# Cached pages split on VectorE instead of ScalarE and VectorE, two pairs ahead, in a hybrid decoder step

## The chip, the cores and the metric

The kernel runs on one core of a Trainium2 chip. The core has a matrix engine (TensorE, PE in the profile; PEld is its loading of stationary weights), VectorE (DVE), ScalarE (ACT), GpSimd (POOL) and a queue engine (SP); POOL and SP issue DMAs here. Each engine works through its own list of instructions in order and waits at an instruction until what it needs is there. The metric is the device time of one execution in microseconds (us).

## The reference, cut to what matters

A trunk of two layers is run for a prompt of 512 tokens and for 8 sample sequences of one token. In each layer a projection feeds three mixers, then comes an output projection and a gated feed-forward part. One mixer is latent attention. For the sample sequences it reads a cache of 4096 past positions, 32 pages of 128 positions for each sequence, through a page table. The keys are not cached: each page of 128 latent vectors (256 wide) is multiplied with the 256 x 512 key weights, and each of the 8 heads' 64 columns is normalised by its root mean square.

```python
def mla_attend_sample(q_nope, q_rope, c_all, kr_all, w_uk, w_uv, k_nope_g):
    k_nope = rms_norm(jnp.einsum('blc,chd->blhd', c_all, w_uk), k_nope_g)
    s = (jnp.einsum('bqhd,blhd->bhql', q_nope, k_nope)
         + jnp.einsum('bqhr,blr->bhql', q_rope, kr_all)).astype(jnp.float32) * SM_SCALE
...
    pr = jax.nn.softmax(s, axis=-1).astype(c_all.dtype)
    o_lat = jnp.einsum('bhql,blc->bqhc', pr, c_all)
    return jnp.einsum('bqhc,chd->bqhd', o_lat, w_uv)
```

The prompt's own attention and the gated recurrence are computed at the same time as the pages.

## The kernel before, in words

Products keep float32 accuracy with a faster matrix format (float32r): an operand x is split into a high half, x rounded to float32r, and a low half, x minus the high half, and the product is the sum of three matmuls (high by high, high by low, low by high). `split` (L291) makes both halves: the high one by a copy on ScalarE, unless its argument `e` names another engine, and the low one by a subtraction on VectorE.

Each layer has a stretch in which the 256 pages of the 8 sequences are worked through: `sample` (L1275), a generator that yields once per page. Two pages make a pair. `load` (L1285) requests the two pages of a pair by two DMAs on SP's queue into one tile, ct. `halve` (L1296) splits the tile into cth and ctl; the halves are written in another order of blocks (k, g, t) than they are read (g, k, t), so the output is strided. The product of a page is 12 matmuls (four groups of three, with the key weights' halves wkh and wkl) into two of four PSUM banks (tile pool pk); ScalarE squares the two results into ksq and copies 8 columns of scores (tile s), and VectorE sums the squares by head (ss, L1449). Before the pages of pair pr, the code calls load(pr + NCT) with NCT = 3 and halve(pr + 1); before the first page it loads three pairs and splits pair 0. At the end of each sequence `chain` turns scores into probabilities and multiplies them with the pages in their natural order (nat), which POOL gathers from memory (L1335). POOL also gathers the rotary keys (kr, L1314).

`mixers` (L857) runs the streams beside the pages: at each page it takes a step of the convolution and recurrence (`first_streams`) and one of the prompt's attention (`attend`), at fixed rates, so that the instructions of all of them stand interleaved on each engine, in an order that is fixed when the program is written. In `attend`, scores are computed on PE in one step, their row maximum (pm) on VectorE one step later, the exponential on ScalarE one step after that, and the transposes on PE two steps after VectorE's normalisation. The first pages are set up within `z_phase`, before the last tile of the input projection (z) is taken from its banks and before VectorE's ra, an input of the last normalisation of keys. SBUF tiles of this size come from one pool of 68 buffers (tag t, L245); a new tile waits for the last reader of its buffer.

Of the kernel before, what the change touches and what calls it, by code (L numbers as in the profile page):

```python
# [71 lines left out]
PLAIN = (0, 1, 2, 3)  # L72
NNAT = 6
KEEP = 3
NCT = 3


def constants():
# [150 lines left out]
class Trunk:  # L229
# [1045 lines left out]
    def sample(self):  # L1275
        nc, a, l = self.nc, self.a, self.l
# [8 lines left out]
        def load(i):  # L1285
            if i >= npair or i in raw or i in halves:
                return
            r = self.t("ct")
            for pgi in range(2):
                n = 2 * i + pgi  # L1290
                reg = nc.sync.value_load(self.idx[0:1, n:n + 1], min_val=0, max_val=POOL_N - 1)
                nc.sync.dma_start(out=r[:, pgi * 256:(pgi + 1) * 256],
                                  in_=a['ct'][l][bass.ds(reg, 1)].rearrange("o p c -> (o p) c"))
            raw[i] = r

        def halve(i):  # L1296
            if i >= npair or i in halves:
                return
            load(i)
            r = raw.pop(i)  # L1300
            hi, lo = self.t("cth", F32R), self.t("ctl", F32R)

            v = [x[:, 0:512].rearrange("p (k g t) -> p g k t", k=4, g=2) for x in (hi, lo)]
            self.split(v[0], v[1], r[:, 0:512].rearrange("p (g k t) -> p g k t", k=4, g=2))
            halves[i] = (hi, lo)

        def load_kr(b, gqs):
            if b >= NB:
                return
            if b not in krs:  # L1310
                krs[b] = self.w("kr")
            k = krs[b]
            for gq in gqs:
                nc.gpsimd.indirect_dma_start(  # L1314
                    out=k[:, gq * P:(gq + 1) * P], out_offset=None, in_=a['krt'].rearrange("l n c -> (l n) c"),
                    in_offset=bass.IndirectOffsetOnAxis(ap=self.idx4[:, 8 * b + gq:8 * b + gq + 1], axis=0),
                    element_offset=l * POOL_N * ROPE * PG)

        def set_q(b):
            if b >= NB:  # L1320
                return
            q = self.qabs[:, 0:128].rearrange("p (k b h) -> p k b h", k=2, b=8)[:, :, b, :]
            o = 256 + 264 * (b % 2)
            hv = self.wkh.rearrange("p (k c) -> p k c", k=2)[:, :, o:o + 8]
            lv = self.wkl.rearrange("p (k c) -> p k c", k=2)[:, :, o:o + 8]
            self.split(hv, lv, q)
# [6 lines left out]
        def load_nat(b, i):  # L1333
            n = b * NPG // 2 + i
            nc.gpsimd.indirect_dma_start(  # L1335
                out=nat(b, i)[:, 0:512], out_offset=None, in_=a['cn'].rearrange("l n c -> (l n) c"),
                in_offset=bass.IndirectOffsetOnAxis(ap=self.idx2[:, n:n + 1], axis=0),
                element_offset=l * POOL_N * PG * LAT)
# [77 lines left out]

        for i in range(NCT):
            load(i)
        load_kr(0, range(8))
        set_q(0)  # L1420
        halve(0)
        chains = [self.own_scores()]
        yield
        for b in range(NB):
            s1, ss, sr = self.s("s1"), self.s("ss"), self.s("sr")
            w0 = 256 + 8 * (b % 2)
            qo = 256 if b % 2 else 0
            ko = 0 if b % 2 else 8
            for t in range(NPG):
                n = b * NPG + t  # L1430
                pr = n // 2
                if t % 2 == 0:
                    load(pr + NCT)
                    halve(pr + 1)
                    cur = halves.pop(pr)
                sq = self.t("ksq")
                for hf in range(2):
                    ps = self.pk("k")
                    c0, cn = ((0, 256), (w0, 264))[hf]
                    for kt in range(2):  # L1440
                        o = (2 * kt + t % 2) * P
                        for i, (cx, wx) in enumerate(((cur[0], self.wkh), (cur[0], self.wkl), (cur[1], self.wkh))):
                            self.mm(ps[:, 0:cn], cx[:, o:o + P], wx[:, 528 * kt + c0:528 * kt + c0 + cn],
                                    kt == 0 and i == 0, kt == 1 and i == 2)
                    k0 = ko if hf else 0
                    self.act(sq[:, 256 * hf:256 * hf + 256], ps[:, k0:k0 + 256], AF.Square)
                    if hf:
                        self.act(s1[:, 8 * t:8 * t + 8], ps[:, qo:qo + 8], AF.Copy)
                nc.vector.tensor_reduce(out=ss[:, 8 * t:8 * t + 8], in_=sq[:, 0:512].rearrange("p (h d) -> p h d", d=64),  # L1449
                                        axis=AX.X, op=ALU.add)  # L1450
                if t == 2:
                    set_q(b + 1)
                if b == 0 and t in (6, 8):
                    nc.gpsimd.memset(self.pp2[t == 8][:, 0:1024], 0.0)
                if b == NB - 1 and t == LAST:
                    self.nat_last = [self.t("natl") for _ in range(NPG // 2)]
                    todo.extend((b, i) for i in range(NPG // 2))
                if t == 10:
                    k = krs.pop(b)[:, 0:1024].rearrange("p (x g c) -> p x g c", x=2, g=4)
                    psr = self.ps("sr")  # L1460
                    for gq in range(4):
                        self.mm(psr[32 * gq:32 * gq + 32, 0:256], self.bd[:, 32 * b:32 * b + 32], k[:, :, gq, :])
                    del k
                    srt = self.t("srt")
                    self.act(srt[:, 0:512].rearrange("p (x h d) -> p x h d", x=4, h=2),
                             psr[:, 0:256].rearrange("p (x h d) -> p x h d", x=4, h=1).to_broadcast([P, 4, 2, 64]), AF.Copy)
                if 14 <= t < 22:
                    load_kr(b + 1, [t - 14])
                if t == 12:
                    psr = self.ps("sr")  # L1470
                    for x in range(4):
                        nc.tensor.transpose(psr[:, x * P:(x + 1) * P], srt[:, x * P:(x + 1) * P], self.c(C_ID))
                    src = psr.rearrange("p (x e c g h) -> p x e c g h", x=2, e=2, c=8, g=2)
                    dst = sr.rearrange("p (x c e h) -> p x e c h", x=2, e=2, c=8)
                    for hh in range(2):
                        r = slice(64 * hh, 64 * hh + 64)
                        for x in range(2):
                            self.act(dst[r, x], src[r, x, :, :, hh, :], AF.Copy)
                    psr = srt = src = None
                self.page = n  # L1480
                for _ in range(NPOP):
                    if todo:
                        load_nat(*todo.pop(0))
                chains = [g for g in chains if next(g, self) is not self]
                yield
            if b == 0:
                assert self.sn is not None
            chains.append(chain(b, s1, ss, sr))
# [526 lines left out]
```

## Time and profile before

| what | value |
|---|---|
| time, median of 3 runs | 2197.75 us (2195.72 to 2198.5) |
| time of the profiled execution | 2197.29 us |
| its span, first to last instruction | 2195.2 us |
| busy: PE, PEld, DVE, ACT, POOL | 98%, 92%, 80%, 59%, 20% of the span |
| granted TensorE clock, mean | 0.998 of full speed |

The busy share is that of one execution. Ends of matmuls are modelled, so a stall of PE can be partly hidden in a matmul that looks long; waits of the weight loads are listed beside those of the matmuls. The page stretches lie at about 170 to 700 us (first layer) and 1240 to 1780 us (second layer) of the span.

### The profile page before, as it was taken

The numbers are of one execution on the slowest core, as the hardware profiler recorded it, in microseconds if no ns is written. First come the engines' busy times: TensorE is split into PE (matmuls) and PEld (weight loads), VectorE is DVE, ScalarE is ACT, GpSimd is POOL, SyncE is SP. The second block draws the span as 40 slices with busy tenths as digits, with TensorE's granted clock in tenths as the row PEclk, the third lists the DMA queues.
The fourth block names the chain that finished last, engine by engine and source line by source line (L and its number), as shares of the span: only waits on it lengthen the run. The fifth ranks groups of instructions, "written<-read, shape, count | busy, mean of one in ns | idle before, by whom it ended". The sixth has DMA issues, their size and how long they took to land.

```text
span 2195.2 us, 50795 instructions
## 1 busy us (share of the span) xinstructions
PE 2147.8 (98%) x18330; PEld 2013.3 (92%) x18330; DVE 1760.1 (80%) x3673; ACT 1291.1 (59%) x3364; POOL 436.6 (20%) x470
## 2 busy tenths in 40 slices
PE   8999999999999999999999999999999999999999
PEld 8998888888888999999999988888888889999999
DVE  7778889877676699889777788897776857998895
ACT  6667767677674554444356677676776745444341
POOL 0004334333362000000001134234333610000000
PEclk9999999999999999999999999999999999999999
DMA  5213445453574423333233134445445733333232
GB/s 183 99 49 107 116 129 146 129 148 119 165 227 142 136 84 106 106 110 98 77 103 105 59 96 138 124 134 151 135 130 163 237 120 117 110 106 102 90 104 78
DMA packets 149484, 267.72 MB, mean 122 GB/s; under 512 B 22833, under 2 KB 103090, under 8 KB 149234
## 3 DMA queue, kind: packets, MB, share of 16 engines
q1 hardware_dynamic: 121778, 178.47, 25.7%
q0 software_dynamic: 24576, 75.52, 11.9%
q10 hardware_dynamic: 2880, 10.49, 1.5%
q8 instruction: 145, 2.38, 0.4%
q14 instruction: 105, 0.86, 0.1%
HBM read 259.86 MB, written 4.54 MB: 120 GB/s over the span
## 4 chain that ended last, share of the span: by engine, by line
PE 77%; DVE 12%; ACT 7%; issue 3%; DMA 1%; SPq 0%; POOL 0%; DVEq 0%; POOLq 0%; ACTq 0%
PE k L268 29%; PE b L268 17%; PE pr L268 17%; PE pv L268 3%; PE wo L268 3%; ACT ry L283 2%; PE sc L268 2%; DVE ss L1449 1%; DVE wl L271 1%; PE ov L268 1%; DVE ctl L271 1%; PE gr L268 1%; DVE sl L271 1%; ACT wh L283 1%; DVE z L271 1%
## 5 line engine op out<-in xcount | busy, mean ns | idle before, releaser
L268 PE MATMUL k<-wkh,cth 128*128 128x256 f32 (+1 forms) x2048 | 619.7, 303 | 3.4 <-ACT ksq L283 1.9
L268 PE MATMUL k<-wkh,ctl 128*128 128x256 f32 (+1 forms) x2048 | 581.5, 284 | 7.4 <-DVE ctl L271 7.3
L268 PE MATMUL k<-wkl,cth 128*128 128x256 f32 (+1 forms) x2048 | 578.0, 282 | 0.0
L283 ACT ACTIVATE ksq<-k 128x256 f32<-128x256 f32 x1024 | 378.8, 388 | 273.2 <-PE k L268 269.3
L1449 DVE TENSOR_REDUCE ss<-ksq 128x8 f32<-128x512 f32 x512 | 347.6, 681 | 169.4 <-ACT ksq L283 165.9
L268 PEld LDWEIGHTS k<-wkh,cth 128*128 128x128 f32 x2048 | 385.8, 188 | 54.9 <-ACT s L283 27.4
L268 PEld LDWEIGHTS k<-wkh,ctl 128*128 128x128 f32 x2048 | 385.3, 188 | 12.6 <-DVE ctl L271 11.8
L268 PEld LDWEIGHTS k<-wkl,cth 128*128 128x128 f32 x2048 | 386.1, 189 | 6.5 <-issue 3.8
L1335 POOL DMA_INDIRECT nat<-in_cn,idx x224 | 231.2, 1032 | 517.7 <-PE pv L268 389.9
L268 PE MATMUL b<-fh,wd 128*128 128x260 f32 x1408 | 232.0, 282 | 1.1 <-ACT fh L283 1.1
L271 DVE TENSOR_TENSOR ctl<-ct,cth 128x512 fp32r<-128x512 f32 x256 | 175.8, 687 | 27.4 <-ACT cth L283 26.8
L268 PEld LDWEIGHTS b<-fh,wd 128*128 128x128 f32 x1408 | 195.3, 188 | 1.5 <-ACT fh L283 1.5
L283 ACT ACTIVATE swh<-sw 128x512 fp32r<-128x512 f32 x144 | 90.8, 631 | 133.6 <-DVE sw L271 129.7
L283 ACT ACTIVATE cth<-ct 128x512 fp32r<-128x512 f32 x256 | 163.2, 637 | 1.2 <-DMA ct<-in_ct 1.1
L268 PE MATMUL b<-fl,wd 128*128 128x260 f32 x704 | 141.8, 283 | 0.5 <-DVE fl L271 0.5
L1314 POOL DMA_INDIRECT kr<-in_krt,idx x128 | 132.4, 1034 | 38.6 <-issue 36.4
L268 PE MATMUL b<-hh,wh 128*128 128x260 f32 x640 | 130.7, 285 | 8.0 <-ACT wh L283 7.2
L268 PE MATMUL b<-hl,wh 128*128 128x260 f32 x640 | 130.1, 285 | 0.2 <-DVE hl L274 0.2
L268 PE MATMUL b<-hh,wl 128*128 128x260 f32 x640 | 129.8, 284 | 0.0
L271 DVE TENSOR_TENSOR x<-x,b 128x260 f32<-128x260 f32 x224 | 84.8, 420 | 33.5 <-PE b L268 32.4
L268 PEld LDWEIGHTS b<-fl,wd 128*128 128x128 f32 x704 | 108.4, 188 | 0.9 <-DVE fl L271 0.9
L268 PEld LDWEIGHTS b<-hh,wh 128*128 128x128 f32 x640 | 99.7, 190 | 8.7 <-ACT wh L283 7.2
(346 smaller groups left out, 5209.2 us busy)
## 6 DMA issues: line engine op xcount, KB each, us to landing
ct<-in_ct SPq DMA_DIRECT2D x512, 128.0 KB
wg<-in_w_gate SPq DMA_DIRECT2D x44, 512.0 KB
wu<-in_w_up SPq DMA_DIRECT2D x44, 512.0 KB
wr<-in_w_in SPq DMA_DIRECT2D x40, 512.0 KB
wdr<-in_w_down SPq DMA_DIRECT2D x96, 192.0 KB
wr<-in_w_out ACTq DMA_DIRECT2D x20, 512.0 KB
wdr<-in_w_down SPq DMA_DIRECT2D x16, 256.0 KB
nat<-in_cn,idx POOLq DMA_INDIRECT x224, 3.5
```

The lines of the kernel that those rows point to most:

```text
L268: self.nc.tensor.matmul(out, lhsT, rhs, start=start, stop=stop)
L271: (e or self.nc.vector).tensor_tensor(out=out, in0=a, in1=b, op=op)
L283: self.nc.scalar.activation(out=out, in_=a, func=f, **k)
L1314: nc.gpsimd.indirect_dma_start(out=k[:, gq * P:(gq + 1) * P], out_offset=None, in_=a['krt'].rearrange("l n c -> (l n) c"), in_offset=bass. ...
L1335: nc.gpsimd.indirect_dma_start(out=nat(b, i)[:, 0:512], out_offset=None, in_=a['cn'].rearrange("l n c -> (l n) c"), in_offset=bass.Indirec ...
L1449: nc.vector.tensor_reduce(out=ss[:, 8 * t:8 * t + 8], in_=sq[:, 0:512].rearrange("p (h d) -> p h d", d=64), axis=AX.X, op=ALU.add)
```

## The change

The high halves of the pages are made by VectorE's cast in place of ScalarE's copy; pairs are split two ahead instead of one, and loaded one pair earlier.

```diff
-NCT = 3
+NCT = 4
...
             v = [x[:, 0:512].rearrange("p (k g t) -> p g k t", k=4, g=2) for x in (hi, lo)]
-            self.split(v[0], v[1], r[:, 0:512].rearrange("p (g k t) -> p g k t", k=4, g=2))
+            self.split(v[0], v[1], r[:, 0:512].rearrange("p (g k t) -> p g k t", k=4, g=2), nc.vector)
             halves[i] = (hi, lo)
...
         halve(0)
+        halve(1)
         chains = [self.own_scores()]
...
                 if t % 2 == 0:
                     load(pr + NCT)
-                    halve(pr + 1)
+                    halve(pr + 2)
                     cur = halves.pop(pr)
```

## Rows read from the trace of the kernel before

**Rows 1.** The page's chain that ended last, shares of the span by line.

```profile
PE k L268 29%; PE b L268 17%; PE pr L268 17%; PE pv L268 3%; PE wo L268 3%; ACT ry L283 2%; PE sc L268 2%; DVE ss L1449 1%; DVE wl L271 1%; PE ov L268 1%; DVE ctl L271 1%; PE gr L268 1%; DVE sl L271 1%; ACT wh L283 1%; DVE z L271 1%
```

**Rows 2.** Windows: length, then busy us (instructions) of PE, PEld, DVE, ACT, POOL.

```profile
170.00:300.00 130.00, 122.47 (x987) 110.73 (x988) 107.13 (x225) 93.96 (x308) 51.39 (x60) 1.00 0.42 123
300.00:400.00 100.00, 98.99 (x962) 86.05 (x962) 93.80 (x227) 69.53 (x226) 26.82 (x27) 1.00 0.41 120
...
1240.00:1360.00 120.00, 112.90 (x909) 104.36 (x908) 100.92 (x219) 82.03 (x263) 38.21 (x48) 1.00 0.34 97
1360.00:1500.00 140.00, 138.44 (x1293) 120.66 (x1296) 124.70 (x287) 99.61 (x321) 52.54 (x54) 1.00 0.46 135
...
sum 1070.00, PE 1045.58 PEld 923.35 DVE 847.11 ACT 742.82 POOL 412.01; mean PE 149.37 PEld 131.91 DVE 121.02 ACT 106.12 POOL 58.86
```

**Rows 3.** Waits of the whole span: us in total, times, longest.

```profile
POOL nat L1335 <- PE pv L268: 389.9, 79, 22.6
...
DVE ctl L271 <- ACT cth L283: 26.8, 40, 3.0
...
PEld k L268 <- DVE ctl L271: 11.8, 22, 1.0
...
PE k L268 <- DVE ctl L271: 7.3, 17, 0.8
PEld stat L268 <- DVE sl L271: 7.2, 9, 1.7
...
PEld mx L1365 <- DVE sa L271: 2.3, 2, 1.2
...
PE k L268 <- ACT ksq L283: 1.9, 4, 0.5
```

**Rows 4.** Timeline around one wait: start, length, in brackets the idle time before.

```profile
190.28 0.28 PE L268 MATMUL k<-wkl,cth 128*128 128x256 f32 x1
...
191.32 0.39 PE L268 MATMUL k<-wkh,ctl 128*128 128x256 f32 x1 [0.76 <-DVE ctl L271]
```

**Rows 5.** Groups by form: busy us, mean ns of one, idle time before them.

```profile
L271 DVE TENSOR_TENSOR ctl<-ct,cth 128x512 fp32r<-128x512 f32 x256 | 175.8, 687 | 27.4 <-ACT cth L283 26.8 <-PE k L268 0.2
...
L283 ACT ACTIVATE cth<-ct 128x512 fp32r<-128x512 f32 x256 | 163.2, 637 | 1.2 <-DMA ct<-in_ct 1.1
...
L387 DVE CAST wh<-wr 128x1024 fp32r<-128x1024 f32 x4 | 2.8, 690 | 3.0 <-DMA wr<-in_w_in 3.0
```

**Rows 6.** Timeline of DVE, two instructions in a row.

```profile
145.79 0.43 DVE L278 TENSOR_SCALAR f<-z 128x512 f32<-128x512 f32 x1
146.14 0.42 DVE L280 TENSOR_SCALAR f<-z 128x512 f32<-128x512 f32 x1
```

**Rows 7.** Timeline of the start of the second layer's pages.

```profile
1254.88 6.01 SPq L1292 DMA_DIRECT2D ct<-in_ct  x6
...
1258.78 1.01 POOL L1314 DMA_INDIRECT kr<-in_krt,idx  x1 [0.30 <-issue]
...
1259.53 0.63 ACT L283 ACTIVATE cth<-ct 128x512 fp32r<-128x512 f32 x1 [1.09 <-DMA ct<-in_ct]
1259.68 0.42 DVE L660 COPY kT<-kr 64x520 f32<-64x520 f32 x1
...
1260.72 0.67 DVE L271 TENSOR_TENSOR ctl<-ct,cth 128x512 fp32r<-128x512 f32 x1
...
1261.32 0.75 DVE L271 TENSOR_TENSOR z<-b,rstd 128x260 f32<-128x260 f32 x2
...
1262.44 0.85 ACT L283 ACTIVATE ry<-stat,consts 128x260 f32<-128x260 f32 x2 [2.27 <-DVE ra L280]
...
1265.05 0.61 ACT L283 ACTIVATE cth<-ct 128x512 fp32r<-128x512 f32 x1
1265.57 0.64 ACT L283 ACTIVATE ksq<-k 128x256 f32<-128x256 f32 x2
...
1265.98 0.49 PE L268 MATMUL sc<-kT,ev 128*128 128x128 f32 x2 [1.64 <-ACT ksq L283]
```

## The prediction

> **What bounds the kernel now.** I read the chain that ended last first, then the busy times of the two stretches that the change touches, then the waits by engine, and last the timeline around single waits. The chain is mostly PE's, and its largest line is the k product of the sample pages, 29% of the span [rows 1]: the two page stretches, 170 to 700 us and 1240 to 1780 us, are PE's, and what the change is worth is read there. In them PE is busy 1045.58 of 1070 us, DVE 847.11, ACT 742.82 [rows 2]. The reader is to see how uneven DVE is: from 300 to 400 us it has 6.2 us free in 100, from 1360 to 1500 us 15.3 in 140, from 170 to 300 us 22.9 in 130.
>
> PE's own stalls in those stretches are few, and the one that this change aims at leads the list: the k product waits for a page pair's low half [rows 3]. Its size is read in two ways, 7.3 us in 17 waits by the matmuls and 11.8 us in 22 by the weight loads. Matmul ends are modelled, so I check one wait: the ctl matmul started 1.04 us after the matmul before it [rows 4], where neighbours in this stream start 0.12 us apart (at 1.04 the loss is 0.92); PE's row put it at 0.76, the weight load's at 0.96. So the weight loads' sum is nearer: 11.8 x 0.92 / 0.96 = 11.3 us.
>
> Why the low half is late: it is made one pair (1070 us / 256 pairs = 4.2 us) before its use, on DVE, behind whatever the streams have queued there and behind ACT's copy, for which DVE stood 26.8 us in 40 waits [rows 3].
>
> **The change part by part.** *Removed from ACT:* 256 copies of 637 ns, 163.2 us of busy time [rows 5]. ACT was free 327 us of the 1070, so this pays only where PE waits for ACT: 1.9 us of k product behind ACT's squares [rows 3]. Ends 0 and 1.9; I take 0.9, because a lighter ACT still has the same squares in front of each bank.
>
> *Added to DVE:* 256 casts of 128x512. No such cast with the strided output stands in the trace. From below: a plain 128x512 TENSOR_SCALAR on DVE lasts 0.43 us, and the next instruction starts 0.35 us after it [rows 6]; the plain cast of twice the elements lasts 0.690 us, little more than the 0.687 us of a two-operand instruction of half its elements [rows 5]. From above: the low half's own instruction, same strides and two inputs, starts its follower 0.60 us later (1260.72 to 1261.32) [rows 7]. I take 0.35, because the cast has one input and its nearest kin in operation is the cast row; 0.60 stays as the other end. So DVE gets 256 x 0.35 = 89.6 us and gets back the 26.8 us for which it stood behind ACT's copy, since both halves now come from its own queue: 847 + 90 - 27 = 910 of 1070, 85%.
>
> [...]
>
> *What DVE's extra work hides behind:* its own free time. At 24 casts per 100 us, 300 to 400 us needs 8.4 us and has 6.2: 2.2 us short. 1360 to 1500 us needs 11.7 and has 15.3; 170 to 300 needs 10.9 and has 22.9; 1240 to 1360 needs 10.0 and has 19.1 [rows 2]. Free time that lies in the wrong place doesn't help a queue that is late for a moment, so I take 3.5 us as PE's loss: the 2.2, and about 1.3 for shorter crowded spots. Ends: 0, since streams place a consumer one or two page steps after its producer, and 8. If the cover is gone, what is late next is DVE's pm (the row maximum that ACT's exponential waits for), then ACT's squares behind it in its queue, then the banks of the k product.
>
> *Moved:* the split goes from one pair ahead to two. A low half then has 8.4 us of program between making and use, against the longest wait of 1.0 us seen [rows 3]; I let all 11.3 us go. Ends 7.3 and 11.8.
>
> *The loads:* four pairs are requested before the first page in place of three, two more DMAs on SP's queue per layer at about 1 us each (six took 6.01 us [rows 7]). They stand before the loads of the level masks and the conv state, which are needed some 10 us later. Afterwards each pair is still requested two pairs before its split, so the lead of the DMA is unchanged, and the queue issues as many as before. POOL's queue is not touched.
>
> *The start of a layer's pages* pays. There halve(0) and now halve(1) stand on DVE before the evacuation of the last z tile and before ra, and ACT stands waiting for ra (2.27 us) with its squares of page 0 behind it; PE then waits 1.64 us for a bank that these squares free [rows 7]. New work before ra: cast 0.35, cast 0.35, one more low half 0.60, in all 1.30 us. ACT's copy between ra and the squares goes: 0.52 us (1265.05 to 1265.57). So PE starts the scores 0.78 us later, in two layers 1.6 us; ends 0 and 2.6. DVE waits for no load: the first pair landed at 1259.53, 4.65 us after its first request at 1254.88, the second was requested 2 us later, so it lands at about 1261.5; DVE comes to its cast at 1260.72 + 0.35 + 0.60 = 1261.67.
>
> *Sum*, against the profiled execution's own 2197.29 us (its span of 2195.2 and 2.1 around it; the median of the runs shown, 2197.75, is 0.46 above it): 2197.29 - 11.3 - 0.9 + 1.6 + 3.5 = **2190.2 us**, 0.3% faster. Own range: 2185 (every gain at its upper end, no crowding) to 2194.
>
> **The rivals.** 0.2%, 4.4 us, is about what a measurement of this kernel can tell from no change.
>
> *A. The wait moves.* DVE goes from 79% to 85% of the stretches, its free share from 21% to 15%; other products of DVE for which PE waits, 7.2 us for sl in the statistics and 2.3 us for sa in front of the transposes [rows 3], then grow by about half, 4.8 us. For it: a DVE product was late before each of these. Against: outside 300 to 400 us the free time holds the casts. 2197.29 - 11.3 + 1.6 + 3.5 + 4.8 = 2195.9, no change.
>
> *B. The strided cast takes 0.60 us, and DVE becomes the bound.* Short by 14.4 - 6.2 = 8.2 us in 300 to 400 and 20.1 - 15.3 = 4.8 in 1360 to 1500; the start costs 2 x (1.80 - 0.52) = 2.6. 2197.29 - 11.3 + 13.0 + 2.6 + 4.8 = 2206.4, slower. It decides from a cast of about 0.52 us on. For it: no strided cast was seen. Against: strides cost the low half nothing visible.
>
> *C. POOL's DMA issues and DVE's casts hold each other up.* POOL issues 384 gathers of about 1 us in the 1070 us, so a cast meets one in 37% of cases; half an issue each makes the cast 0.54 us: 6.8 + 2.8 short, start 2.3, 2197.29 - 11.3 + 9.6 + 2.3 + 4.8 = 2202.7, slower. Against: a one-source copy on DVE began at 1259.68 inside an issue of POOL (1258.78, 1.01 us) and took its usual 0.42 us [rows 7]. The other direction, POOL late, is covered: POOL stood 389.9 us for PE before its next gather [rows 3]. [...]
>
> *D. Buffers.* One more ct and one more pair of halves are alive. Counted in the kernel's allocations, at most 61 of 68 buffers are taken when a pair is loaded, and hardly one is reused within two pages of its last reader; with three fewer free, about a hundred in a layer are. About ten of these stand under 1.5 pages behind a DVE reader; at 1 us of wait each, 2190.2 + 10 = 2200, no change or slower.
>
> **How the numbers follow.** Forecast 0.52, A 0.25, B 0.12, C 0.04, D 0.07. The time is the forecast's. 2184 to 2203 holds the forecast, A, C and D and leaves out B and the tails of the others, somewhat under 2 in 10. Faster by over 0.2% (under 2192.9): the forecast but for its upper edge, 0.50. Within 0.2%: that edge, A and half of D, 0.30. Slower: B, C and half of D, 0.20.
>
> **What the changed profile would show.** The wait of the k product for ctl gone from both lists; a DVE cast cth x256 with a mean near 0.43 us and starts 0.35 apart when packed; DVE's wait for ACT's cth gone; DVE at 19.5 of 20 us or more in parts of 300 to 400 us, with ACT waiting longer for pm; PE's first wait for the squares near 2.4 us. A cast of 0.6 us or more, or new PE waits for sl, sa or pm above 5 us in sum, would make it wrong, as would squares that wait for a buffer's last reader.

## The result, and the profile after

| what | before | after |
|---|---|---|
| time, median of 4 runs | 2197.56 us | 2226.33 us (2223.86 to 2227.58) |
| ratio to before, 95% interval | | 1.0128 (1.0115 to 1.014) |
| busy DVE, ACT | 1760.1, 1291.1 us | 1860.3, 1175.3 us |

The change makes the kernel 28.8 us slower; 2190.2 us, a little faster, was forecast, and the range ended at 2203. The profiled execution took 2223.86 us, its span 2222.1.

A part of the 28.8 us goes with TensorE's granted clock: its mean, as a share of full speed, is 0.993 to 0.996 in the four executions of the changed kernel, the lower the longer the execution, and 0.998 in the profiled one of the kernel before. If time went with the clock throughout, the medians (0.9945 and 0.998) would put 7.8 us down to it, an estimate at the upper end that leaves 21. Why the clock was lower is open. The loss doesn't rest on it: e2 below takes 2228 us with a clock of 0.998.

The page's chain that ended last has less of PE and more of VectorE than in [rows 1]: k went from 29% to 24%, ss from 1% to 3%, and cth, which [rows 1] doesn't list, has 1%.

```profile
PE 67%; DVE 21%; ACT 7%; issue 3%; DMA 1%; SPq 0%; POOL 0%; DVEq 0%; ACTq 0%
PE k L268 24%; PE b L268 17%; PE pr L268 16%; DVE ss L1450 3%; PE pv L268 3%; DVE ctl L271 2%; PE wo L268 2%; ACT ry L283 2%; DVE cth L295 1%; PE sc L268 1%; DVE wl L271 1%; DVE qk L271 1%; PE ov L268 1%; DMA wr<-in_w_out 1%; DVE sl L271 1%
```

The page's costliest groups, as [rows 5]. The cast takes 0.431 us, as the plain TENSOR_SCALAR of its size did in [rows 6]. The two rows of the ctl product are the ones to which the first term of the forecast points: 7.3 and 11.8 us of wait [rows 3] are 0.6 and 1.0. In the row of the subtraction, 11.3 us of idle time have no releaser; they come back below.

```profile
L268 PE MATMUL k<-wkh,ctl 128*128 128x256 f32 (+1 forms) x2048 | 580.2, 283 | 0.6 <-DVE ctl L271 0.6
...
L268 PEld LDWEIGHTS k<-wkh,ctl 128*128 128x128 f32 x2048 | 387.0, 189 | 1.0 <-DVE ctl L271 1.0
L1335 POOL DMA_INDIRECT nat<-in_cn,idx x224 | 222.5, 993 | 547.3 <-PE pv L268 426.6
...
L271 DVE TENSOR_TENSOR ctl<-ct,cth 128x512 fp32r<-128x512 f32 x256 | 178.7, 698 | 11.3
...
L295 DVE CAST cth<-ct 128x512 fp32r<-128x512 f32 x256 | 110.4, 431 | 0.0
```

Waits of the whole span, as [rows 3] (us in total, times, longest). The wait that the change aimed at is gone, and others stand in its place: ScalarE's exponential for pm, PE's k for a bank behind that exponential (pr) or behind the squares, and the transposition mx for m.

```profile
ACT pr L283 <- DVE pm L278: 38.3, 36, 3.4
...
PEld k L268 <- ACT pr L283: 12.8, 20, 1.9
...
PE mx L1365 <- DVE m L271: 11.5, 8, 2.4
...
PE k L268 <- ACT pr L283: 8.0, 12, 1.7
...
PEld pt L1220 <- DVE pr L278: 5.2, 6, 1.6
PE k L268 <- ACT ksq L283: 5.0, 7, 1.5
```

The same view of the kernel before has these two for comparison:

```profile
ACT pr L283 <- DVE pm L278: 17.7, 28, 2.9
...
PE mx L1365 <- DVE m L271: 4.1, 6, 1.3
```

The windows that answer to [rows 2] (length, then busy us of PE, PEld, DVE, ACT, POOL). From 300 to 400 us DVE is at 96.11 in place of 93.80, and PE has lost 4.6 us; from 1360 to 1500 DVE is at 130.54 in place of 124.70 and PE has lost 4.7.

```profile
300.00:400.00 100.00, 94.39 (x904) 81.58 (x903) 96.11 (x229) 56.52 (x191) 28.70 (x29) 1.00 0.40 119
...
1360.00:1500.00 140.00, 133.71 (x1230) 116.68 (x1229) 130.54 (x299) 82.86 (x280) 51.65 (x53) 0.99 0.44 129
```

Windows of different kernels don't hold the same pages, so a second reading is better: VectorE sums each page's squares (ss) once, and its start dates the page. This table is worked out from those 512 starts in each trace: by how many us a page comes later than in the kernel before (negative: earlier). The lower rows are experiments, told below.

```
                       first layer, page                   second layer, page
                       0    16    64    80   112   255       0    16    64    80   112   255
after                0.9   3.7   4.3   7.3  10.2  13.4    14.9  17.9  18.8  21.8  27.0  26.5
e2 cast only        -1.5   1.7   4.2   7.2  10.2  14.5    14.7  18.3  20.9  23.9  26.9  30.9
r6b after sum       -0.1   2.1   1.8   3.7   5.1   7.9     9.3  11.8  11.6  13.4  14.9  16.2
e4 a page later      0.4   2.0   1.1   3.0   4.4   3.5     6.1   8.0   7.2   9.0  10.6   9.4
e3 cast late         1.4   2.0   1.2   0.9   1.3   1.2     4.2   5.5   4.8   4.6   5.0   4.4
e1 ahead only        0.7   1.4   0.5   0.3   0.2  -1.2     1.2   1.1   0.4   0.1   0.1  -1.5
r7b copy, spaced    -0.7  -0.4  -1.7  -1.5  -2.1  -3.8    -1.3  -1.4  -2.5  -2.3  -2.8  -5.1
e9 cast, no low     -0.3  -1.6  -2.9  -4.0  -3.8  -3.5    -1.5  -2.5  -3.7  -4.9  -4.5  -5.1
e10 copy, no low    -0.8  -3.0  -4.1  -5.1  -5.3  -6.7    -4.8  -6.8  -7.7  -8.8  -9.0 -10.6
e11 norm on ACT     -0.5   2.0   4.3   7.2  10.3  14.8    16.2  19.1  21.5  24.4  27.7  31.7
```

In the row "after", the lag grows in pages 0 to 16 and 64 to 112, by 0.37 to 0.57 us a pair in 21 of these 32 pairs of either layer, and hardly from 112 on: that is where the casts cost. Two steps of this execution are not the casts' doing. Between pages 232 and 233 of the first layer the lag rises by 2.9 us, beside two DMA issues on ScalarE's queue that took 3.65 us together here and 0.86 in the execution of before. And in pages 104 to 112 of the second layer it grows by 2.1 us, where the first layer has 0.4: there the granted clock (third number from the end) was lower.

```profile
1480.00:1500.00 20.00, 17.63 (x159) 16.16 (x155) 19.43 (x48) 11.77 (x40) 5.08 (x5) 0.93 0.39 117
1500.00:1520.00 20.00, 20.00 (x171) 17.47 (x171) 16.93 (x43) 9.91 (x36) 3.65 (x4) 0.90 0.30 86
```

What happens in the crowded pages is seen in the changed kernel's timeline (start, length, idle time before it):

```profile
314.17 0.42 DVE L295 CAST cth<-ct 128x512 fp32r<-128x512 f32 x1
...
314.69 0.69 DVE L271 TENSOR_TENSOR ctl<-ct,cth 128x512 fp32r<-128x512 f32 x1
...
316.99 0.17 DVE L271 TENSOR_TENSOR m<-m,sn 128x8 f32<-128x8 f32 x1
317.07 0.68 DVE L271 TENSOR_TENSOR sa<-gr,lev 128x512 f32<-128x512 f32 x1
...
317.81 0.27 PE L1365 MATMUL mx<-consts,m 128*8 128x128 f32 x1 [1.52 <-DVE sa L271]
...
320.39 0.15 DVE L278 TENSOR_SCALAR pm<-pm 128x1 f32<-128x1 f32 x1
320.46 0.43 DVE L295 CAST cth<-ct 128x512 fp32r<-128x512 f32 x1
320.57 0.58 ACT L283 ACTIVATE pr<-sc,pm 128x384 f32<-128x384 f32 x1 [3.41 <-DVE pm L278]
```

VectorE has no gap here. The cast and its subtraction stand ahead of m and sa, and PE stands still 1.52 us before mx, until sa has ended (m had ended 0.65 us before); they stand ahead of pm, so ScalarE stands 3.41 us with the squares of the pages behind it. Also to be seen: the subtraction starts 0.52 us after its cast, not 0.35. Its mean over the 256 pairs is 0.475.

### The profile page after: what moved, and what is told of

The parts are those of the page before. It is cut to its first block, busy times and chain, and to the rows that moved or that the text cites. A ratio compares the mean times of both kernels' runs of the same rounds, so it can differ in the third digit from the quotient of the medians.

```text
span 2222.1 us, 50779 instructions
## 1 busy us (share of the span) xinstructions
PE 2154.3 (97%) x18330; PEld 2018.0 (91%) x18330; DVE 1860.3 (84%) x3929; ACT 1175.3 (53%) x3108; POOL 421.8 (19%) x470
## 3 DMA queue, kind: packets, MB, share of 16 engines
q0 software_dynamic: 24576, 75.52, 11.8%
## 4 chain that ended last, share of the span: by engine, by line
PE 67%; DVE 21%; ACT 7%; issue 3%; DMA 1%; SPq 0%; POOL 0%; DVEq 0%; ACTq 0%
PE k L268 24%; PE b L268 17%; PE pr L268 16%; DVE ss L1450 3%; PE pv L268 3%; DVE ctl L271 2%; PE wo L268 2%; ACT ry L283 2%; DVE cth L295 1%; PE sc L268 1%; DVE wl L271 1%; DVE qk L271 1%; PE ov L268 1%; DMA wr<-in_w_out 1%; DVE sl L271 1%
## 5 line engine op out<-in xcount | busy, mean ns | idle before, releaser
L283 ACT ACTIVATE ksq<-k 128x256 f32<-128x256 f32 x1024 | 383.7, 387 | 375.9 <-PE k L268 371.4
L268 PEld LDWEIGHTS k<-wkh,cth 128*128 128x128 f32 x2048 | 387.5, 189 | 71.3 <-ACT s L283 28.8
L1335 POOL DMA_INDIRECT nat<-in_cn,idx x224 | 222.5, 993 | 547.3 <-PE pv L268 426.6
L271 DVE TENSOR_TENSOR ctl<-ct,cth 128x512 fp32r<-128x512 f32 x256 | 178.7, 698 | 11.3
L295 DVE CAST cth<-ct 128x512 fp32r<-128x512 f32 x256 | 110.4, 431 | 0.0
```

The source lines that it names most:

```text
L268: self.nc.tensor.matmul(out, lhsT, rhs, start=start, stop=stop)
L271: (e or self.nc.vector).tensor_tensor(out=out, in0=a, in1=b, op=op)
L283: self.nc.scalar.activation(out=out, in_=a, func=f, **k)
L295: e.tensor_copy(out=hi, in_=src)
L1335: nc.gpsimd.indirect_dma_start(out=nat(b, i)[:, 0:512], out_offset=None, in_=a['cn'].rearrange("l n c -> (l n) c"), in_offset=bass.Indirec ...
```

## The experiments

Each ran beside the kernel before on the same chip; ratios are to it. Two batches met chips on which the kernel before takes 2289 and 2298 us; in e7's execution there, ScalarE's squares stood 32.2 us in 10 waits for something outside the core or a queue that the profile can't name. Of these two only ratios are compared. The granted clock was lower on both (0.978 to 0.993).

**Which part of the change costs.** e1 keeps ScalarE's copy and takes the rest, e2 takes the cast alone, e3 casts on VectorE only from pair 56 (page 112) on.

```diff
 e1 and e3, of the changed kernel
-self.split(v[0], v[1], r[...]..., nc.vector)
+self.split(v[0], v[1], r[...]...)                                     e1
+self.split(v[0], v[1], r[...]..., nc.vector if i >= 56 else None)     e3
 e2, of the changed kernel
-NCT = 4
+NCT = 3
-        halve(1)
-                    halve(pr + 2)
+                    halve(pr + 1)
```

e1_ahead_only: 

> ScalarE's copy is kept; pairs are loaded four and split two ahead, as in the change. Theory 1 (VectorE's load: in spots a few pages long VectorE has nothing free, and each cast put there lengthens the page stream by its own 0.47 us, 8 pairs of pages 64 to 80 for instance, which is the slope of 0.44 to 0.53 us a pair at which the changed kernel falls behind): VectorE gets no work, so no slope; the k product's wait for the low half (11.3 us) goes, the start of the pages pays 1 to 2.5 us: 2186 to 2191 us. Theory 2 (the order: a pair's work two ahead, its block at another place of VectorE's queue, three more buffers alive): the loss of 28 us is here too, 2215 to 2230 us.

Measured: 2196.08 us, 0.9989 (0.998 to 0.9998). No loss, so theory 2 falls; but the gain is 2 us, less than theory 1 said. The same page that stood still for ctl in [rows 4] now stands for something else:

```profile
192.69 0.39 PE L268 MATMUL k<-wkh,cth 128*128 128x264 f32 x1 [0.47 <-ACT pr L283]
```

e2_cast_only: 

> VectorE's cast is kept; pairs are loaded three and split one ahead, as in the kernel before. Theory 1 (VectorE's load): the same 256 casts in the same crowded spots, slope 0.47 us a pair there, and part of the wait of the k product for the low half stays: 2222 to 2240 us. Theory 2 (order and buffers): no loss, 2190 to 2200 us.

Measured: 2228.05 us, 1.0142 (1.0126 to 1.0157), as theory 1 said. With the cast on VectorE, one pair ahead or two makes no difference that the medians show (at an equal clock e2 might be some us the slower); the cast alone brings the loss. What PE waits for is another thing, though: in e2 it is the k product's own halves, with hardly a wait for them left in the changed kernel.

```profile
PE k L268 <- DVE cth L295: 9.3, 15, 1.1
PE k L268 <- DVE ctl L271: 7.2, 38, 0.3
```

That the loss is the same with different products late speaks for VectorE's time as the bound, and not for one wait.

e3_cast_late: 

> As the changed kernel, but VectorE casts only pairs 56 to 127 of a layer (pages 112 on, where the changed kernel's lag is flat); ScalarE copies pairs 0 to 55. Theory 1 with place (a cast costs only where VectorE is full, and that is before page 112): as with ScalarE's copy throughout, 2186 to 2193 us. If each cast costs the same wherever it stands, 72 of 128 pairs still pay: e1's time and 28 x 72/128 = 16 to 20 us more.

Measured: 2199.82 us, 1.0008 (0.9999 to 1.0017): 3.7 us above e1, where equal cost would give 16 to 20 (theory 1's own range lay lower, since it had e1 lower). By the table of lags it falls behind e1 by 1.3 and 1.0 us in pages 112 to 255 of the two layers. So the 144 late casts cost 2 to 4 us, and the 112 early ones most of the rest, about 26 of 30 by the medians.

**Cast and subtraction side by side, or apart.** e4 issues the subtraction one page (the odd one of the pair) later; e6 issues it in the same page, after the sum of squares, which so also moves ahead of the subtraction. e5 moves both, together, to the odd page. e5 and e6 ran three times (e, r, and r with b), the changed kernel itself once more as r_after.

```diff
 e4 and e6, of the changed kernel
-            self.split(v[0], v[1], src, nc.vector)
+            nc.vector.tensor_copy(out=v[0], in_=src)
+            low.append((v[1], src, v[0]))
...
 e4: subtract() does what stands in low
                     cur = halves.pop(pr)
+                else:
+                    subtract()
...
 e6
                                         axis=AX.X, op=ALU.add)
+                subtract()
...
 e5, of the changed kernel
-                    halve(pr + 2)
                     cur = halves.pop(pr)
+                else:
+                    halve(pr + 2)
```

e4_spaced: 

> As the changed kernel, but VectorE's subtraction for the low half is issued one page after its cast, so that other work stands between the two. In the changed kernel the subtraction starts 0.475 us after its cast (mean of 256), not 0.35 us. Theory 1a (it stands waiting for the cast's end): the start after a cast comes down to about 0.35 us; about 21 pairs of a layer lie in full spots, 2 x 21 x 0.125 = 5 us less than the changed kernel: 2218 to 2223 us. If the cast itself holds VectorE for 0.47 us, whatever follows: no change, 2224 to 2228 us.

Measured: 2207.0 us, 1.0037 (1.0024 to 1.0051): 19 us faster than the changed kernel, four times what was expected. The start after the cast did come down (mean 0.368 us where nothing was waited for):

```profile
317.56 0.43 DVE L1312 CAST cth<-ct 128x512 fp32r<-128x512 f32 x1
317.90 0.68 DVE L1463 TENSOR_REDUCE ss<-ksq 128x8 f32<-128x512 f32 x1
```

e5_odd_page: 

> As the changed kernel, but cast and subtraction, still back to back, are issued before the odd page of a pair in place of the even one. The run with the subtraction one page behind its cast was 19 us faster than the changed kernel, where the shorter start after the cast explains about 5. Theory P (the rest comes from where the block of cast and subtraction stands among VectorE's work of the two pages, the even one being fuller): a part of the 19 us shows here, 2212 to 2221 us. Theory D (it comes from the two no longer following each other): no change from the changed kernel, 2223 to 2230 us.

e6_after_sum: 

> As the changed kernel, but the subtraction is issued after the sum of squares of the same page, so that this sum stands between cast and subtraction; both stay in the same page. Theory D (what counts is that the subtraction doesn't directly follow the cast that it reads): the same time as with the subtraction one page later, 2205 to 2211 us. Theory P (what counts is that the block of 1.1 us is spread over two pages): only the shorter start after the cast, about 5 us, 2218 to 2223 us; between the two if both count.

Measured, before at 2289 us: 1.0075 (1.0045 to 1.0106) and 1.0057 (1.0037 to 1.0078). Both theories seem to hold; without the changed kernel on this chip nothing follows.

r_after: 

> The changed kernel again, as the anchor of the three runs beside it; the batch with the subtraction moved ran on a chip where the kernel before takes 2289 us and TensorE's granted clock was 0.985, and has no run of the changed kernel beside it. On the first chip its ratio to the kernel before was 1.0128 (1.0115 to 1.014); the same is expected, 1.011 to 1.015, on a chip with the same time of before.

r5_odd_page: 

> Cast and subtraction back to back before the odd page, again, now beside the changed kernel. Theory P (place among the two pages): ratio to the kernel before 1.006 to 1.010, as on the slower chip (1.0075). Theory D (distance between cast and subtraction): the changed kernel's own ratio, 1.012 to 1.015.

r6_after_sum: 

> The subtraction after the sum of squares of the same page, again, now beside the changed kernel. Theory D: the ratio of the run with the subtraction one page later, 1.0037 (1.003 to 1.006). Theory P: only the shorter start after the cast, 1.010 to 1.012. The slower chip gave 1.0057.

Measured, before at 2298 us: 1.0173 (1.0159 to 1.0187), 1.0136 (1.0119 to 1.0153), 1.0085 (1.0067 to 1.0104). On this chip the change costs more than was expected, and its clock was lower too (medians 0.980 against 0.987 of the kernel before); e6's is 0.981, so that the 20 us between the two aren't the clock's. The distance gives half of the loss back, the odd page a fifth.

r6b_after_sum: 

> Subtraction after the sum of squares of the same page, a third time. Theory D (distance from its cast): 1.003 to 1.006 of the kernel before, as with the subtraction one page later (1.0037). Theory P (place in the two pages): 1.009 to 1.012.

r5b_odd_page: 

> Cast and subtraction back to back before the odd page, a third time. Theory D: the changed kernel's ratio, 1.0115 to 1.014. Theory P: 1.004 to 1.008. On a slower chip it lay 0.0037 below the changed kernel beside it, which would be 1.009 here.

Measured, before at 2197.24 us: 2215.31 us, 1.0084 (1.007 to 1.0098), and 2222.76 us, 1.0118 (1.0102 to 1.0133). The odd page alone can't be told from the changed kernel. r6b lies between the ranges of the two theories. Subtraction after the sum, in the same page, gives 11.0 us by the medians (9.7 by the ratios; 10.6 by the lags of pages 0 to 112, 8.9 with the 1.7 us of the lower clock taken off), and the other 8.3 (10.3) of e4 come only when the subtraction stands in another page. So both theories have a part: the shorter start, where the count agrees (112 pairs before page 112 x (0.475 - 0.373) = 11.4 us), and the subtraction spread to another page. What the earlier sum of squares gives by itself wasn't tried.

**Is it VectorE's time?** e9 is the changed kernel, e10 is e1, both with 55 subtractions a layer left out.

```diff
+            if i >= 56:
+                first.clear()
+            lo = first[0] if first else self.t("ctl", F32R)
...
+            if not first:
+                self.tt(v[1], src, v[0].bitcast(F32), ALU.subtract)
+                if i < 56:
+                    first.append(lo)
```

e9_cast_no_low: 

> The changed kernel, but the subtraction is left out for pairs 1 to 55 of a layer (they use pair 0's low half, so the output is not the reference's): 55 x 0.62 = 34 us less on VectorE against 55 x 0.475 = 26 us more by the casts. Theory 1 (what the casts cost is VectorE's time in pages 0 to 112): the loss is gone, ratio to the kernel before 0.990 to 1.000. Rival (the casts cost by their own product's or the order's lateness, whatever VectorE's load): 1.008 to 1.016.

Measured: 2192.57 us, 0.9973 (0.9961 to 0.9985). The casts are all there, VectorE has 8 us less to do in pages 0 to 112 of a layer than before, and the loss is gone.

e10_copy_no_low: 

> ScalarE's copy, two pairs ahead, with the same 55 subtractions a layer left out: VectorE has 34 us less to do in pages 0 to 112 than in the kernel before, and doesn't stand for the copy. Theory 1 (the wait for the low half, once taken away, was replaced by waits for VectorE's other products, since VectorE was late): now the 11 us show, 0.992 to 0.996. Rival (the time of these pages is PE's own, and the wait was hidden anyway): 0.998 to 1.000, as with the two-pair lead alone (0.9989).

Measured: 2188.18 us, 0.9952 (0.9938 to 0.9965), 9.1 us faster, 7 us more than e1 gained. So a gain near the forecast 11 us is had where VectorE has time. The run doesn't show that all of it is the wait for the low half, since ScalarE's wait for pm fell too, from 17.7 us:

```profile
ACT pr L283 <- DVE pm L278: 11.6, 20, 2.0
```

**Versions that might beat both.** e7 is e1 with the subtraction one page behind ScalarE's copy (three runs), e8 the kernel before with the copy a page ahead of its subtraction, e11 is e7 with the normalisation of the prompt's probabilities on ScalarE.

```diff
+            self.act(v[0], src, AF.Copy)
+            low.append((v[1], src, v[0]))                                   e7, e8, e11
...
-            self.ts(p[:, 0:P * (i + 1)], p[:, 0:P * (i + 1)], m[:, 3:4])
+            self.act(p[:, 0:P * (i + 1)], p[:, 0:P * (i + 1)], AF.Copy, scale=m[:, 3:4])    e11
```

e7_copy_spaced: 

> ScalarE's copy, two pairs ahead, and the subtraction one page behind it. VectorE stood 26.8 us in 40 waits for ScalarE's copy in the kernel before and in the run with ScalarE's copy two ahead; some 14 us of it lie in pages 0 to 112 of the two layers. Theory 1 (VectorE's time in the full spots sets the page stream): these 14 us, or a good part, come off the 2196 us of that run: 2182 to 2192 us. If VectorE isn't what sets the stream: 2194 to 2198 us.

r7_copy_spaced: 

> ScalarE's copy two pairs ahead and the subtraction one page behind it, again. Theory 1 (VectorE's 26.8 us of standing for the copy, 14 us of them in full spots, come off): 0.993 to 0.9975 of the kernel before, as on the slower chip (0.9963). Otherwise 0.998 to 1.000, as with ScalarE's copy two pairs ahead and nothing else moved.

r7b_copy_spaced: 

> ScalarE's copy two pairs ahead, subtraction one page behind it, a third time (0.9963 and 1.0013 on two slower chips), as the base of the run beside it. Theory 1: 0.993 to 0.9975. Otherwise 0.998 to 1.001.

Measured: 0.9963 (0.9945 to 0.9981), 1.0013 (0.9999 to 1.0027) and, with before at 2197.25, 2193.43 us, 0.998 (0.9971 to 0.9989). On two chips a little faster than both kernels, on one not. Only the first of the three lies in theory 1's range; r7b's 4 us, 2 to 3 more than e1's, fall under "otherwise". VectorE's standing for the copy (26.8 us in [rows 3]) is gone, as r7b's group shows, but most of the 14 us that theory 1 counted on didn't come; why is open:

```profile
L271 DVE TENSOR_TENSOR ctl<-ct,cth 128x512 fp32r<-128x512 f32 x256 | 175.4, 685 | 0.1
```

e8_copy_page_early: 

> The kernel before with one thing changed: ScalarE copies a pair's high half one page ahead of VectorE's subtraction, which stays where it is, one pair ahead (three pairs loaded ahead, nothing added at the start of the pages). Theory 1: VectorE's waits for the copy (26.8 us) go as in the run with two pairs ahead, and the start of the pages costs nothing (1 to 2 us less than there), while the k product's wait for the low half shrinks as VectorE is less late: 2181 to 2192 us. Otherwise 2195 to 2199 us.

Measured, before at 2289 us: 1.001 (0.9988 to 1.0032). A miss, by this interval, with PE still waiting 9.0 us in 18 for ctl; in this execution too ScalarE's squares stood for something outside the core (34.7 us in 10 waits), so that a gain of some us isn't excluded.

e11_norm_on_act: 

> As the run beside it, and the normalisation of the prompt's probabilities (64 products with one number a row, 0.40 us each on VectorE) is ScalarE's. VectorE has 22 x 0.40 = 9 us less a layer in pages 0 to 112, ScalarE as much more. Theory 1: 2 to 8 us faster than the run beside it (0.001 to 0.004 less). Rival (ScalarE becomes late with the squares, and so the banks): 0.002 to 0.01 more.

Measured: 2230.9 us, 1.0156 (1.0142 to 1.017), 37 us above the run beside it, nearly twice the rival's upper end. VectorE has 64 instructions less and ScalarE the room, but the exponential's sum goes to VectorE for its reciprocal and back, and ScalarE stands for that, with the squares behind it:

```profile
ACT pr L283 <- DVE pm L1212: 88.4, 59, 3.8
...
PE k L268 <- ACT ksq L283: 26.4, 26, 1.9
```

## Why the prediction was wrong

Its sum was -11.3 - 0.9 + 1.6 + 3.5. **The term that failed is the last, what DVE's extra work hides behind:** 3.5 us, between 0 and 8, was 30 (the changed kernel's 2226.3 less e1's 2196.1; e2 has the same against the kernel before), or some 22 with the upper estimate of the clock taken off. What is late next it had right: pm, then the squares behind the exponential, then the banks. Two steps of its working were wrong.

*The price of a cast.* 0.35 us was read from two instructions that don't depend on each other [rows 6]. The subtraction reads what the cast has just written and starts 0.475 us after it (mean; the median is 0.455, and casts beside POOL's gathers, below, add to the mean); with the sum of squares between them the cast costs 0.373 (r6b). The 11.3 us without a releaser in the subtraction's row are a part of this. The prediction's other end, 0.60, lay too high, and the cast itself took 0.431 as expected.

*Where the free time lies.* The working gave 300 to 400 us a shortfall of 2.2 us and the stretches of 120 to 140 us none, and added "about 1.3 for shorter crowded spots". The kernel before, in two pieces of 10 us that lie in a window counted as free (length, busy PE, PEld, DVE):

```profile
180.00:190.00 10.00, 9.44 (x75) 8.83 (x74) 9.58 (x23) 7.02 (x24) 0.92 (x6) 1.00 0.34 95
190.00:200.00 10.00, 9.18 (x75) 8.15 (x74) 9.74 (x22) 7.54 (x27) 2.48 (x4) 1.00 0.24 71
```

VectorE has 0.68 us free in 20, and five casts need 2.4. Done over the whole of pages 0 to 112 of a layer (56 casts, 26.6 us at 0.475, against some 28 us free in 230), the shortfalls of the first and the second layer add up to 3.4 and 3.5 us in pieces of 115 us, 6.9 and 8.3 in pieces of 20, and 11.3 and 11.7 in pieces of a pair's 4.2 (where the first cut falls moves these by 1 to 2 us). The lag grew by 9.3 and 12.1 there, 10.4 in the second without the lower clock's step. So the size of the loss could have been read from the trace of before, in pieces of a few us, not as long as a stretch. Of the two steps this is the larger: at the prediction's own 0.35 us, pieces of 4.2 already give 7 to 8 us a layer. That 4.2 us is the right length is not shown: cutting a piece in two never makes the sum smaller, the length was chosen after the result, and for r6b, at 0.373 us, the same pieces give 8 to 9 us where its lag grew by 5.2 and 5.6.

*The 11.3 us.* The wait went, as forecast, and with it 2 us. In pages 10, 14 and 36 of either layer PE in e1 waits for a bank behind the exponential in its place (4.0 us in 8 waits, by the matmuls), since VectorE was late with pm as well as with ctl; another 3.2 us are PE's waits for fh in the feed-forward part, which rose from 1.1 to 4.3 us, for which the change shows no reason. e10, where VectorE has 34 us less to do in a layer, has 9.1 us. The term assumed that nothing else was late by as much.

*ACT lighter, 0.9.* ScalarE's busy time fell by 116 us and PE's wait behind the squares rose from 1.9 to 5.0 us. No gain shows: the squares stand behind the exponential, which waits for VectorE.

*The start of the pages, 1.6.* The lag of page 0 is 0.9 us, and 1.4 arise between the layers: 2.3, in the term's bounds (0 to 2.6). That is luck as far as the rows show: PE's first wait for the squares, through which the term was to act, did not grow from 1.64 us to 2.4 in the second layer but fell, and how much of the 1.4 stands ahead of the pages is open.

```profile
1280.91 0.49 PE L268 MATMUL sc<-kT,ev 128*128 128x128 f32 x2 [1.51 <-ACT ksq L283]
```

**The rivals.** A, the wait moves, had the mechanism, with 0.25 of the chance and 4.8 us in place of 30; it named sl, which stayed (5.4 and 5.3 us by the matmuls), and sa, which grew a little, and the larger parts were pm, m and pr. B fell by its condition (0.431 us, against 0.52 from which it decides) and was nearer in its result, 2206.4: VectorE did become the bound, with a cast that took its usual time. D falls: e1 has the same buffers and loses nothing. C falls as a cause of the loss, but what it speaks of is there: of the 256 casts, 134 stand beside no instruction of POOL and none of them lasts over 0.430 us (mean 0.419), while 116 overlap a gather's issue, with a mean of 0.446 and up to 0.614. That is 116 x 0.027 = 3.1 us of VectorE's time in all; C had a price of 0.19 us for each cast, 49 us, which no run shows. The longest, with the gather beside it:

```profile
562.94 0.95 POOL L1335 DMA_INDIRECT nat<-in_cn,idx  x1 [0.30 <-issue]
563.52 0.61 DVE L295 CAST cth<-ct 128x512 fp32r<-128x512 f32 x1
```

POOL's gathers of nat for their part took 0.993 us on the mean, 1.032 in the kernel before.

**The signs.** Of what the changed profile was to show, three came: the wait for ctl gone, the cast's 0.43 us, ScalarE waiting longer for pm (17.7 to 38.3 us). Two did not: starts 0.35 us apart (0.475) and a longer first wait for the squares. VectorE reached 19.5 us of 20 in one part of 300 to 400 us, and 18.4 to 19.4 in the other four.

## What to carry to other kernels

Free time of an in-order engine counts only near the place where the new work stands: before work is moved to the engine that is busier in the crowded spots, cut the trace into short pieces, about as long as the lead of the products that others wait for, subtract the new work from each, and add up the shortfalls. Several lengths of piece give a range, not a forecast; here pieces of 20 us gave 15 us for both layers, pieces of 4.2 gave 23, and 21 were lost in these pages. A wait that is removed is worth only what the next product of the same late engine leaves of it, here 2 us of 11.3 (e1). And here two instructions that depend on each other cost more side by side than apart; an unrelated one between them, and the second in the next step of the program, gave 19 us of the 30 back.

## What the runs showed of the hardware

The subtraction, which reads the cast's result, started 0.475 us after the cast (mean of 256 in the changed kernel; median 0.455). After the same cast an instruction that doesn't read it started after 0.336 us (median of the sums of squares in e4 and r6b that waited for nothing); that the follower's kind isn't the reason is borne out by two independent TENSOR_TENSOR on z in e9, at 0.336 too. Side by side, then, the follower that reads the result started 0.12 us later, by the medians.

The strided cast of one fp32 source took 0.431 us on the mean, no more than the plain TENSOR_SCALAR of the same size [rows 6]; beside no instruction of POOL it took 0.419, and the plain copy kT of 64x520 0.426 in the kernel before. So no cost of the strides shows here. In the changed kernel 29 casts began 0.20 to 0.37 us before a gather's issue on POOL ended; each of them ended 0.24 to 0.26 us after that issue, and so lasted 0.449 to 0.614 us. The 41 casts that lay wholly within an issue took 0.420 us on the mean, like those beside none (0.419).

In the kernel before, a float32r matmul of the k product (128x256 out) started 0.118 us before the next one of that product, a float32 matmul of the prompt's scores with the same output (sc, from kT and ev) 0.216 us before the next of the scores (medians of 3072 and of 16).
